# Sums of blocks of w_down kept in HBM, and 20 of 44 groups of the down product by seven block products

## The chip, the cores and the metric

The kernel runs on one core of one Trainium2 chip. The metric is the device time of one execution in microseconds. The engines are named as the profile names them: PE (TensorE; PEld its weight loads), DVE (VectorE), ACT (ScalarE), POOL (GpSimd), SP (SyncE, which here issues nearly all loads). ACTq and SPq are the instruction queues of ACT and SP as issuers of DMAs.

## The reference

One block of a transformer on 256 rows (S) of 2048 columns (D), in float32: three kinds of attention side by side, gated and merged, then a feed-forward part with a short causal convolution.

```python
h = rms_norm(x, g_mix)
proj = h @ w_in                        # fq fk fv f_logit | sq sk sv | mq | gates
o_fox = forgetting_attention(...)      # 6 heads
o_sb = stick_breaking_attention(...)   # 6 heads
o_mem = memory_attention(...)          # 4 heads, keys and values from mem @ w_mem_kv
g = sigmoid(gates.reshape(b, s, 3, D) + b_gate)
merged = g[:, :, 0] * (o_fox @ w_br_fox) + g[:, :, 1] * (o_sb @ w_br_sb) + g[:, :, 2] * (o_mem @ w_br_mem)
x = x + merged @ w_out
h2 = rms_norm(x, g_ffn)
u = causal_depthwise_conv(h2 @ w_up, conv_w, conv_b)
u_gate, u_val = split(u, 2)            # 5632 columns each
x = x + (silu(u_gate) * u_val) @ w_down
```

The change concerns the last line, the product of a = silu(u_gate) * u_val (256 x 5632) with w_down (5632 x 2048).

## The kernel before

Every float32 operand of a product is split into a high part and a low part of the type that TensorE takes (hi by a cast on ACT, lo by a subtraction on DVE), and each product is three matmuls: high by high, low by high, high by low. Weights come in pieces of 128 x 1024 (512 KB): a load on SP's queue into a tile raw (four buffers, WBUFS), a cast into hi on ACT (L135, in the down stage L825), a subtraction into lo on DVE (L136, L826), four buffers each (SBUFS).

The stages, in order: keys and values of the memory; the projections by w_in, for the memory queries (mq), the forgetting heads (f0 to f4), the stick-breaking heads (s0 to s4); then for four blocks of 512 columns the three gates (g) and three branch products (b); the product by w_out (o, four blocks); the product by w_up with the convolution (u); the product by w_down (x and y). All but u and the down stage go through product (L150), which takes two k tiles at a time and calls tick (L99) after each two. Work of the heads and transposes is written as generators, put in a queue by later (L96); a tick steps up to two of them (WINDOW), and so the small work is written into the order between the pieces of the large products. The instructions' final order on each engine is set by a planner when the program is built, from this order and its own costs; only where keep_in_program_order is called is it kept as written. On the chip each engine and each queue then runs in order.

The down stage (L776 to L925) takes w_down in two halves of 1024 columns (nb = 0, 1; PIECE = 1024) and the 44 k tiles in 22 pairs p, so 44 groups. A group by eight (eight, L840; letter e in the plans) loads two pieces and makes eight block products of 128 rows by 512 columns: two k tiles, two row tiles t, two column halves n. A group by seven (seven, L855; letter s) makes seven block products out of sums, after Strassen and Winograd: sums of blocks of a, held in sf (FS1 to FS4, made by forms, L791, once per pair for both halves), and sums of blocks of the weights (T1 to T4). With b00, b01 the two halves of the first k tile's piece and b10, b11 those of the second, DVE makes T1 = b00 + b01, T3 = b11 + b01, T2 = T1 + b11, T4 = T2 + b10 (L860, L861, L865, L870). The products go to the accumulators X (four banks) and Y (four banks); gather (L878) adds the Y banks into the residual xres after the last group by seven of a half. Each half ends with the addition of X to xres and the store of the output (L924, L925).

The plans of before (L897) are "eeee" + "see" * 5 + "eee" for the first half and "eee" + "se" * 7 + "eeeee" for the second: 5 and 7 groups by seven, 12 in all. The groups by seven use pairs from 0 on, the others the pairs behind them. forms is called after groups by eight (L913). The pool dn (L776 to L783: tiles raw, ts) is opened at the first call of sums and takes the memory of the convolution's pool (uv.close), so its first user waits for the last convolution. load (L808) goes round six tiles: four of wp, one of dn, one of xt_pool (tag xu).

```python
def tick():
    while waiting and len(active) < WINDOW:
        active.append([waiting.popleft(), 0])
```

Of the kernel before, what the change touches and what calls it, by code (L numbers as in the profile page):

```python
# [40 lines left out]
def hybrid_block(  # L41
# [54 lines left out]
    def later(gen):  # L96
        waiting.append(gen)

    def tick():  # L99
        while waiting and len(active) < WINDOW:  # L100
            active.append([waiting.popleft(), 0])
        for a in list(active):
            if a[1] > 0:
                a[1] -= 1
                continue
            try:
                a[1] = next(a[0]) or 0
            except StopIteration:
                active.remove(a)
# [7 lines left out]
    def finish():  # L117
        while waiting or active:
            tick()
# [345 lines left out]


# [311 lines left out]
    def sums(name, tag="ts"):  # L778
# [4 lines left out]
        return dn[0].tile([P, 1024], F32, tag=tag, name=name)  # L783

    ov = out[0].rearrange("(t p) d -> p t d", p=P)
    dv = w_down[0].rearrange("(k p) n -> p k n", p=P)
    NF = 7
    FS2, FS4, FS3, FS1 = range(4)
    sf = xt_pool.tile([P, NF, 4, 2, P], F32R, tag="xt", name="sf")

    def forms(p):  # L791

        v = aT[:, 2 * p : 2 * p + 2, :].bitcast(F32).rearrange("p k (l t q) -> p k l t q", l=2, t=NT)
        w = sums(f"fw_{p}")
        d = w[:, :512].rearrange("p (f l q) -> p f l q", f=2, l=2)
        r = w[:, 512:].rearrange("p (f q) -> p f q", f=4)
        nc.vector.tensor_tensor(d[:, 0], v[:, 0, :, 0], v[:, 0, :, 1], ALU.subtract)
        nc.vector.tensor_tensor(d[:, 1], v[:, 1, :, 1], v[:, 0, :, 1], ALU.subtract)
        nc.vector.tensor_tensor(r[:, :2], v[:, :, 0, 0], v[:, :, 1, 0], ALU.add)
        nc.vector.tensor_tensor(r[:, 2:], d[:, :, 0], d[:, :, 1], ALU.add)  # L800
        nc.vector.scalar_tensor_tensor(r[:, FS2], r[:, FS1], -1.0, r[:, FS2], ALU.mult, ALU.subtract)
        nc.vector.tensor_tensor(r[:, FS4], r[:, FS4], r[:, FS2], ALU.add)
        nc.scalar.copy(sf[:, p, :, 0], r)
        nc.vector.tensor_tensor(sf[:, p, :, 1], r, sf[:, p, :, 0].bitcast(F32), ALU.subtract)
# [3 lines left out]
    def load(k, n0):  # L808
        name = f"raw_d{n0}_{k}"
        loads[0] += 1  # L810
        at = loads[0] % (WBUFS + 2) if loads[0] > 10 else 0
        if at < WBUFS:
            raw = wp.tile([P, PIECE], F32, tag="raw", name=name)
        elif at == WBUFS:
            raw = sums(name, "raw")
        else:
            raw = xt_pool.tile([P, PIECE], F32, tag="xu", name=name)
        nc.sync.dma_start(raw, dv[:, k, n0 : n0 + PIECE])
        return raw
# [17 lines left out]
    def f_of(p, f):  # L837
        return sf[:, p, f, 0], sf[:, p, f, 1]
# [16 lines left out]
    def seven(p, n0, X, Y, first, last):  # L855
        k0, k1 = 2 * p, 2 * p + 1
# [3 lines left out]
        nc.vector.tensor_tensor(t[:, :512], b00, b01, ALU.add)  # L860
        nc.vector.tensor_tensor(b01, b11, b01, ALU.add)  # L861
        B00, T3 = parts(raw0, f"d{n0}_{k0}")
        three(Y[0], *a_of(k0, 0), B00, first, last)
        three(Y[3], *f_of(p, FS3), T3, first, last)
        nc.vector.tensor_tensor(t[:, 512:], t[:, :512], b11, ALU.add)  # L865
# [4 lines left out]
        nc.vector.tensor_tensor(b10, t[:, 512:], b10, ALU.add)  # L870
        T1, T2 = parts(t, f"t_{n0}_{p}")
        three(Y[2], *f_of(p, FS1), T1, first, last)
        three(Y[1], *f_of(p, FS2), T2, first, last)
        (T4,) = parts(b10, f"t4_{n0}_{p}")
        three(X[1][0], *a_of(k1, 1), T4)
        tick()

    def gather(n0, Y):  # L878
# [3 lines left out]
        w = sums(f"e_{n0}")  # L882
# [14 lines left out]
    plans = ("eeee" + "see" * 5 + "eee", "eee" + "se" * 7 + "eeeee")  # L897
    formed = 0
    for nb, plan in enumerate(plans):
# [4 lines left out]
        for i, c in enumerate(plan):  # L904
            if c == "s":
                seven(s, n0, X, Y, s == 0, s == ns - 1)
# [50 lines left out]
```

## Time and profile before

| | |
|---|---|
| time, median of 3 runs | 1492.08 us (1490.9 to 1492.4) |
| the profiled execution: its own time | 1490.28 us |
| its span | 1488.6 us |
| DMA | 283.62 MB, mean 191 GB/s |
| q1 (SP's queue) | 280.26 MB, 62.2% of the 16 engines |
| q10 (ACT's queue) | 2.11 MB, 0.4% |
| stretch of the down stage in the span | from 1252.5 us to the end |

A row of a view by lines has: line of the kernel, engine, operation, names (out<-in), shapes, count, then busy time in us and mean ns of one, then the idle time of the engine just before these instructions with what ended it. A row of the timeline has: start in us, duration in us, engine, line, operation, names, shapes, count and, in brackets, idle time before it with its releaser. A row of a table of stretches has: the stretch, its length, then the busy time and count of PE, PEld, DVE, ACT, POOL, then the granted clock of TensorE as a share, the busy share of the 16 DMA engines and their GB/s. A row of waits has: who waited for whom, us in total, times, longest. A row of DMA issues has: names, queue, count, KB of each, median us from issue to landing. A matmul's duration is from its start to its modelled end, and the next one starts before that end.

### The profile page before, as it was taken

Reading aid. Unit: us, or ns where it says so; the run is one execution under the profiler, and the core shown is the slowest. Engines: PE = TensorE matmul, PEld = TensorE weight load, DVE = VectorE, ACT = ScalarE, POOL = GpSimd, SP = SyncE. Lnnn points to the kernel's source line nnn. Section 1 sums busy time; section 2 is a strip of 40 time slices with the busy share of each in tenths; the row PEclk is TensorE's granted clock in tenths of the full one; section 3 lists DMA queues with packets and bytes.
Section 4 is the critical chain, followed back from the end, with each engine's and each line's share of the span. In section 5 each row is a group of like instructions: output and inputs, shape, how many; then the busy total and the mean of one; then the engine's idle time right before and its main releaser. Section 6 shows DMA issues by size and latency. Waiting matters only on the chain.

```text
span 1488.6 us, 19873 instructions
## 1 busy us (share of the span) xinstructions
PE 1481.9 (100%) x7430; PEld 1254.8 (84%) x7430; DVE 1016.9 (68%) x1457; ACT 791.9 (53%) x1100; POOL 16.2 (1%) x46
## 2 busy tenths in 40 slices
PE   9999999999999999999999999999999999999998
PEld 7888888888888888888888888888888888888887
DVE  5766566555655646556557778777778777898885
ACT  6755454458544444444456556556556556454552
POOL 0000000001000000000000000000000000000000
PEclk9999999999999999999999999999999999999999
DMA  9675475474666666655566666666666666666663
GB/s 309 200 200 159 125 224 157 119 223 152 192 196 207 190 206 203 185 192 189 185 179 182 204 186 184 197 187 183 199 194 185 194 189 197 192 206 217 214 205 114
DMA packets 138814, 283.62 MB, mean 191 GB/s; under 512 B 9290, under 2 KB 18398, under 8 KB 138718
## 3 DMA queue, kind: packets, MB, share of 16 engines
q1 hardware_dynamic: 137390, 280.26, 62.2%
q10 hardware_dynamic: 1328, 2.11, 0.4%
q8 instruction: 58, 0.95, 0.3%
q14 instruction: 38, 0.31, 0.1%
HBM read 280.23 MB, written 2.10 MB: 190 GB/s over the span
## 4 chain that ended last, share of the span: by engine, by line
PE 97%; ACT 1%; DVE 1%; POOL 0%; issue 0%; DMA 0%; SPq 0%; DVEq 0%; POOLq 0%
PE u L762 22%; PE u L763 11%; PE g L146 5%; PE g L148 5%; PE g L147 5%; PE x L832 4%; PE x L831 4%; PE x L830 4%; PE s L146 2%; PE s L148 2%; PE s L147 2%; PE f L146 2%; PE f L148 2%; PE f L147 2%; PE o L147 2%; PE o L148 2%
## 5 line engine op out<-in xcount | busy, mean ns | idle before, releaser
L762 PE MATMUL u<-hT,hi_u 128*128 128x512 f32 x1232 | 428.4, 391 | 0.0
L763 PE MATMUL u<-hT,lo_u 128*128 128x256 f32 x1232 | 345.0, 280 | 0.0
L136 DVE TENSOR_TENSOR lo_u<-raw_u,hi_u 128x1024 fp32r<-128x1024 f32 x176 | 215.4, 1224 | 115.2 <-ACT hi_u L135 115.1
L762 PEld LDWEIGHTS u<-hT,hi_u 128*128 128x128 f32 x1232 | 230.4, 187 | 50.5
L135 ACT CAST hi_u<-raw_u 128x1024 fp32r<-128x1024 f32 x176 | 184.8, 1050 | 139.0 <-PE u L762 112.6
L763 PEld LDWEIGHTS u<-hT,lo_u 128*128 128x128 f32 x1232 | 232.8, 189 | 0.0
L136 DVE TENSOR_TENSOR lo_g<-raw_g,hi_g 128x1024 fp32r<-128x1024 f32 x96 | 117.6, 1228 | 104.8 <-ACT hi_g L135 102.2
L135 ACT CAST hi_g<-raw_g 128x1024 fp32r<-128x1024 f32 x96 | 100.8, 1052 | 130.7 <-PE g L147 107.2
L146 PE MATMUL g<-hi_g,xT 128*128 128x512 f32 x336 | 132.2, 393 | 0.0
L148 PE MATMUL g<-lo_g,xT 128*128 128x512 f32 x336 | 131.0, 390 | 0.0
L147 PE MATMUL g<-hi_g,xT 128*128 128x512 f32 x336 | 130.8, 389 | 0.0
L825 ACT CAST hi_d<-raw_d 128x1024 fp32r<-128x1024 f32 x88 | 90.0, 1051 | 64.2 <-PE x L831 29.2
L826 DVE TENSOR_TENSOR lo_d<-raw_d,hi_d 128x1024 fp32r<-128x1024 f32 x88 | 105.8, 1222 | 21.6 <-ACT hi_d L825 19.9
L832 PE MATMUL x<-lo_d,aT 128*128 128x512 f32 x268 | 104.3, 390 | 0.1
L831 PE MATMUL x<-hi_d,aT 128*128 128x512 f32 x268 | 104.3, 389 | 0.0
L830 PE MATMUL x<-hi_d,aT 128*128 128x512 f32 x268 | 104.3, 389 | 0.0
L148 PEld LDWEIGHTS g<-lo_g,xT 128*128 128x128 f32 x336 | 63.1, 188 | 13.4
L147 PEld LDWEIGHTS g<-hi_g,xT 128*128 128x128 f32 x336 | 63.1, 188 | 12.7
L146 PEld LDWEIGHTS g<-hi_g,xT 128*128 128x128 f32 x336 | 63.1, 188 | 12.7
L136 DVE TENSOR_TENSOR lo_s<-raw_s,hi_s 128x1024 fp32r<-128x1024 f32 (+1 forms) x40 | 44.7, 1118 | 37.1 <-ACT hi_s L135 37.1
L136 DVE TENSOR_TENSOR lo_f<-raw_f,hi_f 128x1024 fp32r<-128x1024 f32 (+1 forms) x40 | 44.7, 1119 | 34.5 <-ACT hi_f L135 33.0
L135 ACT CAST hi_f<-raw_f 128x1024 fp32r<-128x1024 f32 (+1 forms) x40 | 38.6, 968 | 52.4 <-PE f L147 47.6
(358 smaller groups left out, 2797.4 us busy)
## 6 DMA issues: line engine op xcount, KB each, us to landing
raw_u<-in_w_up_dram SPq DMA_DIRECT2D x176, 512.0 KB, 4.2
raw_g<-in_w_in_dram SPq DMA_DIRECT2D x96, 512.0 KB, 3.7
raw_d<-in_w_down_dram SPq DMA_DIRECT2D x88, 512.0 KB, 5.0
raw_f<-in_w_in_dram SPq DMA_DIRECT2D x32, 512.0 KB, 3.7
raw_s<-in_w_in_dram SPq DMA_DIRECT2D x32, 512.0 KB, 3.7
raw_o<-in_w_out_dram SPq DMA_DIRECT2D x32, 512.0 KB, 4.3
raw_kv<-in_w_mem_kv_dram SPq DMA_DIRECT2D x15, 512.0 KB, 5.0
raw_b<-in_w_br_fox_dram SPq DMA_DIRECT2D x12, 512.0 KB, 4.8
```

The source lines that it names most:

```text
L135: pin(nc.scalar.copy(hi[:, :m], raw[:, :m]))
L136: pin(nc.vector.tensor_tensor(lo[:, :m], raw[:, :m], hi[:, :m].bitcast(F32), ALU.subtract))
L146: pin(nc.tensor.matmul(o, lhsT=xh, rhs=wh, start=first, stop=False))
L147: pin(nc.tensor.matmul(o, lhsT=xl, rhs=wh, start=False, stop=False))
L148: pin(nc.tensor.matmul(o, lhsT=xh, rhs=wl, start=False, stop=last))
L762: nc.tensor.matmul(ps[i], lhsT=hi[:, j, c], rhs=hT(k + j), start=first, stop=False)
L763: nc.tensor.matmul(ps[i][:, :S], lhsT=lo[:, j, c], rhs=hT(k + j)[:, :S], start=False, stop=last)
L825: nc.scalar.copy(hi[:, :n], src)
L826: nc.vector.tensor_tensor(lo[:, :n], src, hi[:, :n].bitcast(F32), ALU.subtract)
L830: nc.tensor.matmul(o, lhsT=ah, rhs=w[0], start=first, stop=False)
L831: nc.tensor.matmul(o, lhsT=al, rhs=w[0], start=False, stop=False)
L832: nc.tensor.matmul(o, lhsT=ah, rhs=w[1], start=False, stop=last)
```

## The change

Twenty groups are done by seven products, ten in each half. Their weight sums T1 to T4 are no longer made in the down stage: a generator weight_sums makes them from the stage of the memory queries on and stores them in 20 tiles in HBM (kept, 128 x 4 x 512 float32, 1 MB each). It is stepped once by every tick outside finish. For each tile it works in two halves of 256 columns: two loads of 256 KB on ACT's queue into a tile pre (one buffer), two steps on, three DVE operations (one of 128 x 512, two of 128 x 256), one step on a store of 512 KB on ACT's queue, and two steps more. A half so takes five steps, all of it 200.

seven now loads five blocks on SP's queue: b00 and T3 into one raw tile, the second k tile's piece into another, T1 and T2 into a third, T4 into a tile of sm (tag junk, two buffers). It has no sums on DVE any more. forms is called where the plan has an f; it has four sums on DVE (one of 512 columns, one of 256, two of 128), two casts on ACT and two differences on DVE. FS1 is stored in aT, in the place of the block of a that no product needs any longer; sf holds the other three, 28 in its main tile and two in a tile of dn.

```diff
-    def tick():
+    background = []
+
+    def tick(beside=True):
+        if beside and background:
+            next(background[0], None)
@@
     def finish():
         while waiting or active:
-            tick()
+            tick(beside=False)
@@
+    plans = ("efefeff" + "ssef" * 2 + "sseff" * 2 + "sseeeee", "ee" + "sse" * 5 + "eeeee")
+    dram = ctx.enter_context(tc.tile_pool(name="dram", bufs=1, space=bass.MemoryType.DRAM))
+    dv = w_down[0].rearrange("(k p) n -> p k n", p=P)
+    T1, T3, T4, T2 = range(4)
+    sums_of = {}
+
+    def weight_sums(pool):
+        for nb, plan in enumerate(plans):
+            for p in range(plan.count("s")):
+                kept = dram.tile([P, 4, 512], F32, tag=f"kept_{nb}_{p}", name=f"kept_{nb}_{p}")
+                for h in range(2):
+                    w = pool.tile([P, 4, 256], F32, tag="pre", bufs=1, name=f"pre_{nb}_{p}_{h}")
+                    n0 = nb * PIECE + h * 256
+                    for n in range(2):
+                        nc.scalar.dma_start(
+                            w.rearrange("p (k n) c -> p k n c", k=2)[:, :, n],
+                            dv[:, 2 * p : 2 * p + 2, n0 + n * 512 : n0 + n * 512 + 256],
+                        )
+                    yield
+                    yield
+
+                    both = w[:, 1:2].to_broadcast([P, 2, 256])
+                    nc.vector.tensor_tensor(w[:, 0:2], w[:, 0:4:3], both, ALU.add)
+                    nc.vector.tensor_tensor(w[:, T2], w[:, T1], w[:, T2], ALU.add)
+                    nc.vector.tensor_tensor(w[:, T4], w[:, T2], w[:, T4], ALU.add)
+                    yield
+                    nc.scalar.dma_start(kept[:, :, h * 256 : (h + 1) * 256], w)
+                    yield
+                    yield
+                sums_of[nb, p] = kept
@@ behind weighted, ahead of the projection of the memory queries
+    background.append(weight_sums(gp))
@@ behind the product by w_out
+    assert next(background.pop(), None) is None
     mix.close()
@@ forms
-        nc.vector.tensor_tensor(d[:, 0], v[:, 0, :, 0], v[:, 0, :, 1], ALU.subtract)
-        nc.vector.tensor_tensor(d[:, 1], v[:, 1, :, 1], v[:, 0, :, 1], ALU.subtract)
-        nc.vector.tensor_tensor(r[:, :2], v[:, :, 0, 0], v[:, :, 1, 0], ALU.add)
-        nc.vector.tensor_tensor(r[:, 2:], d[:, :, 0], d[:, :, 1], ALU.add)
-        nc.vector.scalar_tensor_tensor(r[:, FS2], r[:, FS1], -1.0, r[:, FS2], ALU.mult, ALU.subtract)
-        nc.vector.tensor_tensor(r[:, FS4], r[:, FS4], r[:, FS2], ALU.add)
-        nc.scalar.copy(sf[:, p, :, 0], r)
-        nc.vector.tensor_tensor(sf[:, p, :, 1], r, sf[:, p, :, 0].bitcast(F32), ALU.subtract)
+        nc.vector.tensor_tensor(w[:, :512].rearrange("p (k c) -> p k c", k=2), v[:, :, 0], v[:, :, 1], ALU.add)
+
+        a10 = w[:, P : 2 * P].unsqueeze(1).to_broadcast([P, 2, P])
+        nc.vector.tensor_tensor(r[:, FS3 : FS1 + 1], w[:, :512].rearrange("p (f q) -> p f q", f=4)[:, 0:4:3], a10, ALU.subtract)
+        nc.vector.scalar_tensor_tensor(r[:, FS2], r[:, FS1], -1.0, a[:, 0, 0], ALU.mult, ALU.subtract)
+        nc.vector.tensor_tensor(r[:, FS4], r[:, FS2], a[:, 1, 0], ALU.add)
+        at = 3 * p
+        if at + 3 <= NX:
+            groups = [(sf[:, at : at + 3], r[:, :3])]
+        else:
+            groups = [(s_of(p, f), r[:, f]) for f in range(3)]
+        groups.append((s_of(p, FS1), r[:, FS1]))
+        for dst, src in groups:
+            nc.scalar.copy(dst[..., 0, :], src)
+        for dst, src in groups:
+            nc.vector.tensor_tensor(dst[..., 1, :], src, dst[..., 0, :].bitcast(F32), ALU.subtract)
@@ seven
-        raw0, raw1 = load(k0, n0), load(k1, n0)
-        t = sums(f"t_{n0}_{p}")
-        b00, b01, b10, b11 = raw0[:, :512], raw0[:, 512:], raw1[:, :512], raw1[:, 512:]
-        nc.vector.tensor_tensor(t[:, :512], b00, b01, ALU.add)
-        nc.vector.tensor_tensor(b01, b11, b01, ALU.add)
+        kept = sums_of[nb, p]
+        raw0 = raw_tile(f"raw_d{n0}_{k0}")
+        nc.sync.dma_start(raw0[:, :512], dv[:, k0, n0 : n0 + 512])
+        nc.sync.dma_start(raw0[:, 512:], kept[:, T3])
+        raw1 = load(k1, n0)
+        raw2 = raw_tile(f"raw_t{n0}_{p}")
+        nc.sync.dma_start(raw2.rearrange("p (n c) -> p n c", n=2), kept[:, 0:4:3])
+        raw3 = sm.tile([P, 512], F32, tag="junk", bufs=2, name=f"raw_t4_{n0}_{p}")
+        nc.sync.dma_start(raw3, kept[:, T4])
@@
-        nc.vector.tensor_tensor(t[:, 512:], t[:, :512], b11, ALU.add)
@@
-        nc.vector.tensor_tensor(b10, t[:, 512:], b10, ALU.add)
-        T1, T2 = parts(t, f"t_{n0}_{p}")
+        T1w, T2w = parts(raw2, f"t_{n0}_{p}")
@@
-    plans = ("eeee" + "see" * 5 + "eee", "eee" + "se" * 7 + "eeeee")
@@ the loop over a plan
+            elif c == "f":
+                forms(formed)
+                formed += 1
             else:
                 eight(e, n0, X, i == 0, i == len(plan) - 1)
                 e += 1
-                if e >= 2 and s < ns and formed <= (s if nb == 0 else ns - 1):
-                    forms(formed)
-                    formed += 1
```

More of the change, by code (lines that the diff above doesn't have):

```diff
@@ L776, in hybrid_block, with place @@
     dn = []
-    def sums(name, tag="ts"):
+    def place(shape, dt, tag, name):
         if not dn:
@@ new lines, in hybrid_block, with s_of @@
+    NX = 28
+    sf = xt_pool.tile([P, NX, 2, P], F32R, tag="xt", name="sf")
+    sf_rest = []
+    def s_of(p, f):
+        if f == FS1:
+            return aT[:, 2 * p].rearrange("p (l t q) -> p l t q", l=2, t=NT)[:, :, 1]
+        at = 3 * p + f
+        return sf[:, at] if at < NX else sf_rest[0][:, at - NX]
+    def forms(p):
+        if 3 * p + 3 > NX and not sf_rest:
+            sf_rest.append(place([P, 2, 2, P], F32R, "rest", "sf_rest"))
+        v = aT[:, 2 * p : 2 * p + 2, :].bitcast(F32).rearrange("p k (l c) -> p k l c", l=2)
+        w = place([P, PIECE], F32, "ts", f"fw_{p}")
+        a = w[:, :512].rearrange("p (k t q) -> p k t q", k=2, t=NT)
+        r = w[:, 512:].rearrange("p (f q) -> p f q", f=4)
+        nc.vector.tensor_tensor(w[:, :512].rearrange("p (k c) -> p k c", k=2), v[:, :, 0], v[:, :, 1], ALU.add)
[13 more added lines that the diff above has]
+            nc.vector.tensor_tensor(dst[..., 1, :], src, dst[..., 0, :].bitcast(F32), ALU.subtract)
@@ L806, in hybrid_block, with raw_tile @@
     loads = [0]
-    def load(k, n0):
-        name = f"raw_d{n0}_{k}"
+    def raw_tile(name):
         loads[0] += 1
@@ L812, in load @@
         if at < WBUFS:
-            raw = wp.tile([P, PIECE], F32, tag="raw", name=name)
+            return wp.tile([P, PIECE], F32, tag="raw", name=name)
         elif at == WBUFS:
-            raw = sums(name, "raw")
-        else:
-            raw = xt_pool.tile([P, PIECE], F32, tag="xu", name=name)
+            return place([P, PIECE], F32, "raw", name)
+        return xt_pool.tile([P, PIECE], F32, tag="xu", name=name)
+    def load(k, n0):
+        raw = raw_tile(f"raw_d{n0}_{k}")
         nc.sync.dma_start(raw, dv[:, k, n0 : n0 + PIECE])
@@ L869, in seven @@
         tick()
-        nc.vector.tensor_tensor(b10, t[:, 512:], b10, ALU.add)
-        T1, T2 = parts(t, f"t_{n0}_{p}")
[L872 to L875, printed above, removed]
+        T1w, T2w = parts(raw2, f"t_{n0}_{p}")
+        three(Y[2], *f_of(p, FS1), T1w, first, last)
+        three(Y[1], *f_of(p, FS2), T2w, first, last)
+        (T4w,) = parts(raw3, f"t4_{n0}_{p}")
+        three(X[1][0], *a_of(k1, 1), T4w)
         tick()
@@ L881, in gather @@
         xr = lambda t, n: xres[:, t, n0 + n * 512 : n0 + (n + 1) * 512]
-        w = sums(f"e_{n0}")
+        w = place([P, PIECE], F32, "ts", f"e_{n0}")
         e, f = w[:, :512], w[:, 512:]
```

22 lines of the change are left out of this document (9 added, 13 removed).

## Prediction

> **What bounds the kernel now.** First the page: busy shares and the chain of waits.
>
> ```profile
> PE 1481.9 (100%) x7430; PEld 1254.8 (84%) x7430; DVE 1016.9 (68%) x1457; ACT 791.9 (53%) x1100; POOL 16.2 (1%) x46
> ...
> PE 97%; ACT 1%; DVE 1%; POOL 0%; issue 0%; DMA 0%; SPq 0%; DVEq 0%; POOLq 0%
> ```
>
> The chain is TensorE for 97% of the span. A busy PE proves little, since matmuls overlap, so the next view is the timeline of PE in the down stage: its first matmul, the first group by seven, the group behind it, and the last matmul.
>
> ```profile
> 1252.49 0.39 PE L830 MATMUL x<-hi_d,aT 128*128 128x512 f32 x1
> ...
> 1274.29 0.39 PE L830 MATMUL y<-hi_d,aT 128*128 128x512 f32 x1
> ...
> 1279.28 0.39 PE L830 MATMUL x<-hi_d,aT 128*128 128x512 f32 x1
> ...
> 1484.20 0.39 PE L832 MATMUL x<-lo_d,aT 128*128 128x512 f32 x1
> ```
>
> Four groups by eight of 24 matmuls lie between the first two rows: 21.80 us / 96 = 0.2271 us for each (the 0.39 is a latency). The stage has 32 groups of 24 and 12 of 21, 1020 matmuls: 1020 x 0.2271 = 231.6 us. From 1252.49 to the last start and one matmul more are 231.9 us, so PE loses 0.3 us there, most of it in the first group by seven (4.99 us where 21 x 0.2271 = 4.77). The time of this stage is its count of matmuls. Whether that still holds with fewer depends on the other resources, by stretch (engines, clock, DMA share, GB/s):
>
> ```profile
> 10.00:20.00 10.00, 9.65 (x48) 7.81 (x49) 6.31 (x10) 6.06 (x12) 0.00 (x0) 1.00 1.04 381
> 340.00:690.00 350.00, 349.70 (x1571) 289.36 (x1570) 203.89 (x212) 166.76 (x172) 7.89 (x16) 1.00 0.65 192
> 1250.00:1480.00 230.00, 229.94 (x1017) 189.71 (x1016) 193.78 (x251) 116.82 (x131) 0.00 (x0) 1.00 0.59 195
> ```
>
> The clock is granted in full. In the down stage VectorE is busy 84% (193.78 of 230) and is the second limit. The DMA engines have moved 381 GB/s where they were asked to.
>
> **The change, part by part.**
>
> *Fewer products.* Eight more groups by seven, each without one product of three matmuls: 8 x 3 x 0.2271 = **-5.45 us** on the path that sets the end. The matmuls that stay have the same shapes. Nothing can gain more: the stage loses only 0.3 us.
>
> *VectorE in the down stage.* Durations by form:
>
> ```profile
> L826 DVE TENSOR_TENSOR lo_d<-raw_d,hi_d 128x1024 fp32r<-128x1024 f32 x83 | 99.7, 1222 | 16.9 <-ACT hi_d L825 15.2
> L860 DVE TENSOR_TENSOR t<-raw_d 128x512 f32<-128x512 f32 x12 | 8.3, 691 | 1.8 <-DMA raw_d<-in_w_down_dram 1.5
> L826 DVE TENSOR_TENSOR lo_t<-raw_d,hi_t 128x512 fp32r<-128x512 f32 x12 | 8.3, 688 | 1.5 <-ACT hi_t L825 1.5
> L804 DVE TENSOR_TENSOR sf<-fw,sf 128x512 fp32r<-128x512 f32 x7 | 4.8, 690 | 2.8 <-ACT sf L803 2.8
> L797 DVE TENSOR_TENSOR fw<-aT 128x256 f32<-128x256 f32 x7 | 3.0, 424 | 0.2
> L801 DVE SCALAR_TENSOR_TENSOR fw<-fw 128x128 f32<-128x128 f32 x7 | 2.0, 288 | 0.1
> ```
>
> A group by seven costs VectorE 3 x 1.22 + 0.69 + 4 sums of 0.69 = 7.1 us now and 4.35 us after, since the four sums come from HBM; a group by eight 2 x 1.22 = 2.44. A call of forms costs 4 x 0.42 + 2 x 0.29 + 0.69 = 2.95 now; after, 0.69 + 0.42 + 2 x 0.29, then differences over 384 and 128 columns (0.55 and 0.29, between the rows for 512 and 256, and as 128) = 2.53. Calls go from 7 to 10. A repeat "ss e f" then has 2 x 4.35 + 2.44 + 2.53 = 13.7 us of VectorE beside 66 x 0.2271 = 14.99 us of PE; "ss e ff" has 16.2, 1.2 us too much, in two repeats. Against that stands a lead:
>
> ```profile
> 1245.38 1.23 DVE L826 TENSOR_TENSOR lo_d<-raw_d,hi_d 128x1024 fp32r<-128x1024 f32 x1 [1.55 <-ACT hi_d L825]
> ...
> 1252.06 0.77 DVE L735 TENSOR_TENSOR cr<-cr,u 128x256 f32<-128x256 f32 x2
> ...
> 1266.75 0.43 DVE L168 TENSOR_TENSOR aT<-y,aT 128x256 fp32r<-128x256 f32 x1 [0.47 <-ACT aT L167]
> 1267.21 0.43 DVE L797 TENSOR_TENSOR fw<-aT 128x256 f32<-128x256 f32 x1
> ...
> 1269.00 0.29 DVE L802 TENSOR_TENSOR fw<-fw 128x128 f32<-128x128 f32 x1
> 1270.04 0.69 DVE L804 TENSOR_TENSOR sf<-fw,sf 128x512 fp32r<-128x512 f32 x1 [0.74 <-ACT sf L803]
> ...
> 1278.19 0.69 DVE L826 TENSOR_TENSOR lo_t<-raw_d,hi_t 128x512 fp32r<-128x512 f32 x1
> 1278.80 0.42 DVE L799 TENSOR_TENSOR fw<-aT 128x256 f32<-128x256 f32 x1
> 1279.14 2.36 DVE L826 TENSOR_TENSOR lo_d<-raw_d,hi_d 128x1024 fp32r<-128x1024 f32 x2
> ```
>
> The first lo_d is ready at 1246.61 and PE takes it at 1252.49: 5.9 us of lead, what four pairs of hi and lo buffers allow. It covers 2 x 1.2 us if regained between; bounds 0 and 2.4, I take **+0.5**.
>
> *The first group by seven comes earlier.* It stands behind three groups by eight, not four: at 1252.49 + 72 x 0.2271 = 1268.84, and its second product needs the low part of FS3 0.9 us later, at 1269.75. Forms can't start before the last convolution frees the memory of pool dn: 1266.75 + 0.43 = 1267.2 now, with VectorE full since 1252.06, and the same after, as nothing ahead of it changes. Of the first call the six sums took 2.1 us, the wait for ACT's copy 0.75, the difference 0.69; with 1.7 us of sums (some 1.55 as they overlap) and 0.55 it ends at 1270.06, 0.3 us late: the lower bound. Upper: four calls now stand ahead of that group, 10.1 us, and if VectorE did all four first, the parts of both groups that remain (1.22 + 0.69 + 4.35) would end at 1267.2 + 16.4 = 1283.6, where PE wants the last at 1268.84 + 42 x 0.2271 - 0.45 = 1277.9: 5.7 us. The last rows above show lo parts slipped in between the dependent operations of a call, so I take **+1.2**: 0.3 and most of one such part (1.22).
>
> *Sums made ahead.* 20 tiles of 1 MB in halves: 40 times two loads and a store on ACT's queue and three operations on VectorE (0.69 + 2 x 0.42 = 1.53 us; 61 us in all). A half takes 5 of the 248 ticks of the products; 200 are needed, so they end in the last quarter of the gates. A tick is 12 matmuls, 2.73 us.
>
> ```profile
> 408.31 1.05 ACT L135 CAST hi_g<-raw_g 128x1024 fp32r<-128x1024 f32 x1 [1.67 <-PE b L147]
> 448.47 1.23 DVE L136 TENSOR_TENSOR lo_g<-raw_g,hi_g 128x1024 fp32r<-128x1024 f32 x1 [1.50 <-ACT hi_g L135]
> L925 ACTq DMA_DIRECT2D out_dram<-xres x9: 338/338/445, 1367.0 to 1485.5; - x9
> raw_g<-in_w_in_dram SPq DMA_DIRECT2D x96, 512.0 KB, 3.7
> raw_d<-in_w_down_dram SPq DMA_DIRECT2D x88, 512.0 KB, 5.0
> ```
>
> Both engines idle over 1.5 us for each piece, 7.5 us in five ticks, against 1.53 us on VectorE and 3 x 0.338 = 1.0 us of issuing on ACT. Three waits are added. VectorE's sum waits for its load: behind it stand the lo parts. ACT's store waits for that sum, and its next load for the store, since tile pre has one buffer: behind both stand the hi casts. Each has two ticks, 5.5 us, or one; transfers of 512 KB land in 3.7 to 5.0 us. A wait that overruns by a microsecond falls into the 5.9 us of lead, which is the cover; without it each of 40 would cost its overrun. It is gone in one place:
>
> ```profile
> 334.00:352.00 18.00, 17.85 (x85) 14.68 (x84) 10.07 (x14) 16.69 (x21) 3.04 (x5) 1.00 0.50 149
> ...
> PEld r L626 <- POOL sb L603: 1.1, 2, 0.6
> ```
>
> Here a pair of stick-breaking heads keeps ACT busy 93%, and PE waits for its mask (0.15 us of idle PE in this window). A second pair does the same some 27 us later. Lower bound 0 if the issues fall outside, upper 7 us a pair (a rival below); I take **+0.4** for all of the stages ahead, one issue in each pair's stretch.
>
> *Traffic.* Ahead of the down stage 1.05 MB each five ticks (13.6 us), 77 GB/s on top of 192: at 192 / 0.65 = 295 GB/s for a full share that is 0.91, so it fits. In the down stage a group by seven reads 1.75 MB (1.835 million bytes), five blocks in rows of 2 KB, one of 4 KB, in 4.77 us: 385 GB/s; "ss e" 4.72 million bytes in 14.99 us, 315, below the 381 of the table. Eight buffers of raw pieces lie between. Taken: 0; upper bound with the rivals. SP's load of a T4 waits for the lo of the T4 two groups before, and the next weights stand behind it; that lies 10 us or more ahead, hence nothing. The stores of the sums ended some 600 us earlier.
>
> [...]
>
> **Sum.** -5.45 + 1.2 + 0.5 + 0.4 = -3.35 us. The profiled execution took 1490.28 (span 1488.6 and 1.7 around it), 1.8 under the median 1492.08; against the median: **1488.7 us**.
>
> **Rivals.** *Forms hold PE at the head of the down stage*: the upper bound 5.7 in place of 1.2 and 0.5 becomes 1.5: -5.45 + 5.7 + 1.5 + 0.4 = +2, or with half of it, -1: 1491 to 1494, no change. For it: VectorE full from 1252. Against: the lo parts slipped in.
>
> *DMA bounds the pairs.* At the full-share rates, 295 GB/s for rows of 2 KB and 195 / 0.59 = 331 for 4 KB, a seven takes 1.311 / 295 + 0.524 / 331 = 6.03 us and an eight 3.17, "ss e" 15.2 us against 15.0: nine times 0.2, and twice 1.3 where the buffers run dry, some 4 us: 1492. Against it: 381 GB/s at a share of 1.04, so that the share overstates. [...]
>
> *Slower: ACT's queue in the stretches of the stick-breaking heads.* A pair's stretch of 27 us holds two halves, six issues (2.0 us) and two waits of a store for sums (1.53 each, and about 1 of landing beyond two ticks): up to 7 us of ACT, on a chain that PE already waits for. At 5.2 us a pair: -5.45 + 1.7 + 10.4 = +6.7: 1498.7. It decides from 3.4 us a pair.
>
> *Slower: the DMA engines full at the gates.* If rows of 1 KB cost as much each as rows of 2 KB, a half takes 7.1 of its 13.6 us, 0.52 on top of 0.65: 17% too much over 112 ticks (305 us), +52 us. At half of that, in proportion to the bytes, it is 0.26 and all fits; it decides from some 4.8 us for a half, where 0.65 + 0.35 is 1.
>
> **How the numbers follow.** Forecast 0.43, forms 0.18, DMA in the pairs 0.10, ACT's queue 0.20, full engines 0.09. A measurement of this kernel tells 0.2%, 3 us, from no change. Faster: the forecast but for its upper end, 0.39. Same: that end and the two rivals about zero, 0.32. Slower: 0.29. The forecast's own range is 1486.8 (every cost at its lower bound, with 0.3 off) to 1490. The whole range reaches from 1486.3 to 1500, which leaves out the full engines and the worst of ACT's queue.
>
> **What would show it.** PE in the down stage: 996 matmuls, 226.2 us, with a gap of about a microsecond at the first group by seven, behind sf; small gaps at lo in "ss e ff". The raw loads there at some 270 GB/s, with no wait of ACT for a raw_d. In the stages ahead PE without new gaps but at L626. Wrong if PE waits for lo_g or hi_g in the gates, if DMA stands behind raw tiles in the pairs, or if the gap ahead of the first pair exceeds 3 us.

## The result, and the profile after

The changed kernel took 1557.37 us (median of four runs, 1555.95 to 1558.11) beside 1492.19 us for the kernel before (four runs, 1490.9 to 1492.4): a ratio of 1.0442 with a 95% interval of 1.0429 to 1.0455, 65 us slower. The profiled execution took 1556.67 us with a span of 1554.9, 66.3 us longer than the span before. The page of the changed kernel, busy shares, one queue and the chain of waits:

```profile
PE 1504.7 (97%) x7406; PEld 1262.5 (81%) x7406; DVE 1051.6 (68%) x1558; ACT 797.4 (51%) x1127; POOL 16.8 (1%) x46
...
q10 hardware_dynamic: 44208, 44.06, 8.4%
...
PE 69%; DMA 20%; DVE 5%; ACT 3%; issue 2%; ACTq 1%; DVEq 0%
```

PE has 24 matmuls fewer, as it should, and the chain is PE for only 69% of the span: 20% are transfers, which had 0%. ACT's queue (q10) moves 44 MB where it moved 2.11, which takes 8.4% of the DMA engines. Where the time lies shows from the starts of the stages in PE's timeline (first matmul to first matmul, us):

| stage | before | after | difference |
|---|---|---|---|
| keys and values of the memory, from 0 | 58.9 | 85.5 | +26.6 |
| memory queries | 22.9 | 22.9 | 0 |
| f, forgetting heads | 111.3 | 117.4 | +6.1 |
| s, stick-breaking heads | 113.8 | 125.3 | +11.5 |
| gates and branch products | 365.5 | 391.6 | +26.1 |
| product by w_out, product by w_up | 580.1 | 580.1 | 0 |
| down stage, to the end of its last matmul | 231.9 | 228.0 | -3.9 |

The down stage is 3.9 us shorter; everything lost is lost ahead of w_up, and 26.6 us of it in the first 85 us, ahead of the place where weight_sums is put on the list. Two views say why. The first is the table of stretches (columns as in the prediction), two rows of before and then four of after:

```profile
0.00:112.00 112.00, 109.66 (x514) 87.88 (x515) 74.40 (x124) 71.74 (x130) 1.51 (x10) 1.00 0.75 237
...
307.00:675.00 368.00, 367.70 (x1657) 304.68 (x1656) 215.16 (x227) 181.48 (x193) 11.02 (x24) 1.00 0.65 193
```

```profile
0.00:115.00 115.00, 96.06 (x405) 74.36 (x406) 64.51 (x115) 59.94 (x114) 1.50 (x10) 0.93 0.77 246
115.00:225.00 110.00, 106.86 (x526) 89.69 (x525) 75.28 (x133) 46.20 (x75) 0.00 (x0) 0.98 0.74 227
225.00:350.00 125.00, 119.16 (x587) 99.39 (x587) 79.79 (x147) 52.69 (x89) 3.56 (x12) 0.96 0.78 242
350.00:745.00 395.00, 377.88 (x1666) 307.83 (x1666) 235.12 (x273) 175.05 (x191) 11.77 (x24) 0.99 0.72 221
```

PE stands idle for 18.9, 3.1, 5.8 and 17.1 us there, 45 us together, against some 2.6 in both rows of before, and the granted clock is under 1. A finer table of stretches has twelve windows of 3.41 us at a clock of 0.50, 41 us, which cost about 19 us of work (an estimate: half of the 38 us that PE is busy in them). 42 of idle time and 19 of clock are 61 of the 70 us lost ahead of the down stage; the other 9 aren't told apart here. The second view is that of one tile, pre, in the changed kernel: each row has durations in ns (least, median, most) and the first and the last start in us; below, the waits, with us in total, times and the longest:

```profile
L223 ACTq DMA_DIRECT2D pre<-in_w_down_dram x80: 369/378/691, 1.3 to 534.7; - x80
L231 DVE TENSOR_TENSOR pre<-pre x40: 671/693/773, 7.0 to 539.7; 128x512 f32<-128x512 f32 x40
```

```profile
DVE pre L231 <- DMA pre<-in_w_down_dram: 78.5, 30, 7.1
...
ACT hi_g L139 <- DVE pre L233: 24.3, 6, 5.9
...
ACT sb L671 <- DMA kept<-pre: 12.3, 3, 5.0
...
PE kv L152 <- DVE lo_kv L140: 10.6, 4, 4.4
PE g L152 <- DVE lo_g L140: 10.6, 8, 3.3
```

The first load of pre is issued at 1.3 us, though the ticks that write it start with the memory queries: the planner has moved the sums' operations. VectorE then stands before 30 of the 40 sums until a load lands, 78.5 us in all, with the lo parts behind it; ACT stands at stores until the sums are made, with the hi casts behind it. One such cycle in the gates, in the timeline of ACT, DVE and PE:

```profile
495.10 0.90 ACTq L223 DMA_DIRECT2D pre<-in_w_down_dram  x2
...
498.03 1.98 ACT L139 CAST hi_g<-raw_g 128x1024 fp32r<-128x1024 f32 x2
505.24 0.53 ACTq L235 DMA_DIRECT2D kept<-pre  x1
505.88 1.05 ACT L139 CAST hi_g<-raw_g 128x1024 fp32r<-128x1024 f32 x1 [5.88 <-DVE pre L233]
510.39 0.90 ACTq L223 DMA_DIRECT2D pre<-in_w_down_dram  x2
511.41 2.00 ACT L139 CAST hi_g<-raw_g 128x1024 fp32r<-128x1024 f32 x2 [4.48 <-issue]
```

```profile
497.19 1.23 DVE L140 TENSOR_TENSOR lo_g<-raw_g,hi_g 128x1024 fp32r<-128x1024 f32 x1 [1.05 <-ACT hi_g L139]
502.58 0.69 DVE L231 TENSOR_TENSOR pre<-pre 128x512 f32<-128x512 f32 x1 [4.16 <-DMA pre<-in_w_down_dram]
```

```profile
501.20 0.39 PE L151 MATMUL g<-hi_g,xT 128*128 128x512 f32 x1
504.92 0.69 PE L152 MATMUL g<-lo_g,xT 128*128 128x512 f32 x1 [3.34 <-DVE lo_g L140]
505.41 0.63 PE L150 MATMUL g<-hi_g,xT 128*128 128x512 f32 x1
505.84 0.63 PE L151 MATMUL g<-hi_g,xT 128*128 128x512 f32 x1
```

The load is issued at 495.10. The first sum stands in DVE's order a single lo part later: 4.16 us idle. ACT has made two more hi casts and then stands 5.88 us at the store, whose sums aren't there. PE runs out of lo_g for 3.34 us, and when it goes on its matmuls are 0.43 us apart instead of 0.23, with the granted clock at 0.50 from 505.05 to 508.46. After the store ACT makes one hi cast and stands again, 4.48 us, at the next load. That load takes the one buffer of pre, which the store still reads, so the kernel makes it wait until the store has landed; the profile names no releaser here.

DVE does not pass its wait by: it idles 4.16 us though both hi_g of 498.03 are cast by 500.01, and their lo parts come at 503.65 and 505.12, behind the sum. The 5.88 and the 4.48 us are idle time of ACT itself, in front of its casts.

In the down stage the timeline of PE in the changed kernel (first matmul, first group by seven and its second half, last matmul) reads:

```profile
1322.75 0.39 PE L892 MATMUL x<-hi_d,aT 128*128 128x512 f32 x1
...
1342.22 0.50 PE L892 MATMUL y<-hi_d,aT 128*128 128x512 f32 x1 [0.82 <-ACT hi_d L887]
...
1346.87 0.50 PE L892 MATMUL y<-hi_t,aT 128*128 128x512 f32 x1 [0.41 <-ACT hi_t L887]
...
1550.57 0.39 PE L894 MATMUL x<-lo_d,aT 128*128 128x512 f32 x1
```

From 1322.75 to 1550.57 and one matmul more are 228.05 us; 996 matmuls at 0.2271 are 226.2. The first group by seven has two gaps of 0.82 and 0.41 us, and with what follows them loses 1.9 us; no other place loses over 0.15.

### The profile page after: what moved, and what is told of

The parts are those of the page before. It is cut to its first block, busy times and chain, and to the rows that moved or that the text cites. A ratio compares the mean times of both kernels' runs of the same rounds, so it can differ in the third digit from the quotient of the medians.

```text
span 1554.9 us, 20294 instructions
## 1 busy us (share of the span) xinstructions
PE 1504.7 (97%) x7406; PEld 1262.5 (81%) x7406; DVE 1051.6 (68%) x1558; ACT 797.4 (51%) x1127; POOL 16.8 (1%) x46
## 4 chain that ended last, share of the span: by engine, by line
PE 69%; DMA 20%; DVE 5%; ACT 3%; issue 2%; ACTq 1%; DVEq 0%
PE u L805 21%; PE u L806 11%; DMA kept<-pre 10%; DMA pre<-in_w_down_dram 9%; PE x L892 4%; PE x L893 4%; PE x L894 4%; PE g L152 3%; PE g L150 3%; PE g L151 3%; PE o L150 2%; PE o L152 2%; PE o L151 2%; PE b L152 1%; PE b L151 1%
## 5 line engine op out<-in xcount | busy, mean ns | idle before, releaser
L892 PE MATMUL x<-hi_d,aT 128*128 128x512 f32 x212 | 82.6, 390 | 0.0
L893 PE MATMUL x<-hi_d,aT 128*128 128x512 f32 x212 | 82.5, 389 | 0.0
L894 PE MATMUL x<-lo_d,aT 128*128 128x512 f32 x212 | 82.0, 389 | 0.0
L231 DVE TENSOR_TENSOR pre<-pre 128x512 f32<-128x512 f32 x40 | 27.8, 694 | 80.1 <-DMA pre<-in_w_down_dram 78.5
L139 ACT CAST hi_s<-raw_s 128x1024 fp32r<-128x1024 f32 (+1 forms) x40 | 38.0, 960 | 55.2 <-PE s L151 22.1
L140 DVE TENSOR_TENSOR lo_o<-raw_o,hi_o 128x1024 fp32r<-128x1024 f32 x32 | 39.2, 1225 | 36.8 <-ACT hi_o L139 32.3
```

Source lines behind the costliest of these rows:

```text
L139: pin(nc.scalar.copy(hi[:, :m], raw[:, :m]))
L140: pin(nc.vector.tensor_tensor(lo[:, :m], raw[:, :m], hi[:, :m].bitcast(F32), ALU.subtract))
L892: nc.tensor.matmul(o, lhsT=ah, rhs=w[0], start=first, stop=False)
L893: nc.tensor.matmul(o, lhsT=al, rhs=w[0], start=False, stop=False)
L894: nc.tensor.matmul(o, lhsT=ah, rhs=w[1], start=False, stop=last)
```

## The experiments

My theory after the result: what costs is neither the bytes nor the added operations, but engines with one order standing at transfers, because the planner put load, sum and store closer together than a transfer takes. Rivals: the traffic itself; the added work on ACT and DVE; the down stage. The kernel before took 1490.4 to 1490.9 us in the runs beside these experiments; ratios are to it.

**The two halves of the change, each alone.** In the first kernel the down stage is that of the change, but reads plain blocks of w_down of the same sizes; the sums T1 to T4 are left out.

```diff
-    background.append(weight_sums(gp))
@@ seven
-        nc.sync.dma_start(raw0[:, 512:], kept[:, T3])
+        nc.sync.dma_start(raw0[:, 512:], dv[:, k0, n0 + 512 : n0 + 1024])
```

> weight_sums is left out; the down stage of the changed kernel reads blocks of w_down of the same sizes in place of the kept sums (the sums T1 to T4 are left out). If the down stage gives what its matmuls say less its stalls (5.45 - 1.7), the time is 1487 to 1489.5 us with a down stage of 228 us. If part of the loss lies in the down stage, by its 35 percent more traffic, it is above 1492 us.

1487.14 us, ratio 0.9976 (0.9966 to 0.9985): 3.6 us faster. The second has weight_sums of the change and the down stage of before, which makes its own sums:

> weight_sums as in the changed kernel, with nobody reading the sums; down stage of the kernel before. If the whole loss stands ahead of the w_up stage: 1558 to 1564 us, 69 us above the kernel before. If it takes both parts together, under 1540 us.

1563.11 us, ratio 1.0483 (1.0462 to 1.0504). So the down stage brings what it was forecast to bring, and the whole loss lies in weight_sums.

**The order.** The operations of weight_sums are kept where the ticks write them:

```diff
+    keep = tc.keep_in_program_order
-                        nc.scalar.dma_start(
+                        keep(nc.scalar.dma_start(
@@ and the same around its three sums and its store
```

> Every operation of weight_sums is kept in the written order of its engine; traffic, sums and the down stage are those of the changed kernel. If the planner's moving them to the head of the queues, with ACT and DVE standing at transfers that land later than planned, is the cause, most of the 65 us go: 1488 to 1500 us, the first stage 59 us long again, no wait of DVE for pre over 3 us. If the 42 MB of added traffic starve the weight loads whatever the order, the time stays above 1530 us.

1503.08 us, ratio 1.0087 (1.0072 to 1.0102): 54 of the 65 us are gone, and the first stage takes 59.2 us, where it took 58.9 before and 85.5 in the change. But 16 us are left against the down stage alone, and the time lies 3 us above the expected range. In the waits of DVE and PE in this kernel, and in PE's timeline where a pair of stick-breaking heads runs:

```profile
DVE pre L233 <- DMA pre<-in_w_down_dram: 15.5, 9, 3.0
```

```profile
PE r L669 <- POOL sb L647: 3.7, 2, 1.9
PE fa L599 <- DVE fx L594: 2.1, 1, 2.1
PE tpm L533 <- DVE sm L498: 1.9, 2, 1.6
```

```profile
358.50 0.70 PE L669 MATMUL r<-sb,after 128*128 128x256 f32 x2 [1.90 <-POOL sb L647]
359.73 0.80 PE L670 MATMUL r<-sb,ones 128*128 128x128 f32 x2 [0.53 <-POOL sb L647]
```

A second pair has the same gaps some 31 us later (1.85 and 0.53). Behind the first the granted clock is 0.51 from 359.4 to 362.8 us, and its mean from 300 to 400 us, where both pairs lie, is 0.97. PE's waits for weights are small, 0.6 us for lo_f and 0.5 for lo_kv (0.5 before). What it waits for are tiles of the heads: of the memory heads (tpm), which run beside the stage f, of the forgetting heads (fa) beside s, of the stick-breaking heads (r) in the gates. These three stages are 4.6, 2.6 and 8.1 us longer than before.

With only ACT's loads and stores kept in order, and the three sums free:

> Only ACT's loads and stores of weight_sums are kept in the written order; the three sums on DVE may be moved. If it is ACT's queue that blocks, the time is that of the run with all kept, within 3 us. If DVE's standing at its load blocks too, the sums are still put right behind the planned landing and the time lies 5 us or more above that run.

1510.9 us, ratio 1.0142 (1.0121 to 1.0162), DVE's wait for the loads 49.1 us: 7.8 us more than with all of it kept. With the order free again, but weight_sums written in only behind the stick-breaking heads:

```diff
-    background.append(weight_sums(gp))
@@ the first block of gates, behind the heads
+            background.append(weight_sums(gp))
```

> weight_sums is written into the order only after the stick-breaking heads (what is left is drained ahead of the w_up stage), and nothing keeps its operations there. If the planner takes them forward to wherever their buffer is free, whatever the ticks say, the first load still stands at the head of ACT's queue and the time is above 1530 us. If the ticks' place counts, it is 1500 us or less.

1559.09 us, ratio 1.0462 (1.0432 to 1.0493): as the change itself. Its first load again is one of the first instructions on ACT. Where the unpinned work was written didn't count here.

**The traffic.** The fixed order, but the three sums left out, and stores of the same size that read rows of xres and so wait for no load:

```diff
-                    keep(nc.vector.tensor_tensor(w[:, 0:2], w[:, 0:4:3], both, ALU.add))
@@ the other two sums likewise
-                    keep(nc.scalar.dma_start(kept[:, :, h * 256 : (h + 1) * 256], w))
+                    keep(nc.scalar.dma_start(kept[:, :, h * 256 : (h + 1) * 256], xres[:, 0, :1024].rearrange("p (f c) -> p f c", f=4)))
```

> All kept in the written order, but the three sums on DVE are left out and the stores read rows of the residual: the same bytes in the same sizes at the same ticks, and no wait between loads, sums and stores but that of one load for the one before. If the 13 us by which the run with all kept is above the kernel before, in spite of the shorter down stage, come from waits in the queues, it is 1487 to 1491 us. If the traffic costs them, it stays at 1500 to 1504 us.

1488.2 us, ratio 0.9985 (0.9976 to 0.9994): the same bytes, queue and ticks cost 1 us over the down stage alone. The 15 us between this and the fixed order are the sums and what stands at them.

**The stick-breaking heads.** The fixed order, not stepped while the first block of gates runs, where these heads lie:

```diff
@@ around the first block of gates
+    held = background.pop()
...
+            background.append(held)
```

> All kept in the written order, and weight_sums is not stepped in the gates of the first block, where the stick-breaking heads run. If ACT's queue in their stretches is a part of the 16 us over the down-only run, as the rival of the prediction has it, the two gaps of 2.4 us at the heads' r matmuls and the two half-clock stretches behind them go: 1494 to 1498 us. If it is nothing, 1503 us again.

1495.56 us, ratio 1.0038 (1.0025 to 1.0051): 7.5 us less, with both pairs of gaps gone. 8.4 us over the down stage alone were left. They lie in f and s, 3.8 and 4.7 us longer than before, where PE waits 1.9 us for tpm and 3.0 for fa. The gates take 365.6 us beside 365.5 before: away from the heads two ticks of room are enough.

**Four ticks for a half: a miss.** weight_sums only in products without heads, what is left of it written in one piece ahead of w_up, and four steps for a half instead of five, by one step fewer between a store and the next load:

```diff
                     keep(nc.scalar.dma_start(kept[:, :, h * 256 : (h + 1) * 256], w))
                     yield
-                    yield
```

> All kept in the written order; weight_sums is stepped only in the products beside which no heads run (memory queries, first forgetting projection, and from the branch products of the first block on), four steps a half in place of five, the rest drained ahead of the w_up stage. If all that is left of the loss lies beside the heads, the stages ahead take what they took before and the time is 1487 to 1489.5 us, below both kernels. If 320 GB/s in the gates starve the weight loads, it is above 1495 us.

1546.1 us, ratio 1.0364 (1.0339 to 1.0388), far slower. ACT's timeline shows what the step was for:

```profile
639.86 0.52 ACTq L237 DMA_DIRECT2D kept<-pre  x1
640.50 1.05 ACT L139 CAST hi_g<-raw_g 128x1024 fp32r<-128x1024 f32 x1 [0.44 <-ACT hi_g L139]
645.34 0.90 ACTq L225 DMA_DIRECT2D pre<-in_w_down_dram  x2
646.36 2.00 ACT L139 CAST hi_g<-raw_g 128x1024 fp32r<-128x1024 f32 x2 [4.80 <-issue]
```

ACT stands 4.80 us ahead of the load. The profile names no releaser, but the load takes the one buffer that the store of 639.86 reads, and it goes out 5.5 us behind that store, about as long as such stores take to land (where POOL issues the loads, in an experiment below, the profile does name the store: 160.4 us in 39 waits):

```profile
kept<-pre ACTq DMA_DIRECT2D x40, 512.0 KB, 5.0
```

(a row of DMA issues of the change). In the gates this kernel takes 390.2 us where the one before it took 365.6, and PE waits 8.0 us for lo_g, so one tick less brings a standstill that the fixed order alone did not have. The traffic isn't the cause there: from 465 to 697 us this kernel moves 260 to 271 GB/s, and the kernel with the fixed order alone moves 277 GB/s from 500 to 600 us with PE full. But the step is only a part: the products by w_out and w_up take 613.7 us instead of 580.1, and the sums written ahead of w_up run beside them until 831 us.

**Another queue: a miss.** Loads and stores are issued by POOL, which is nearly idle (16.8 us busy in the change), so that ACT stands at nothing:

```diff
-                        nc.scalar.dma_start(
+                        nc.gpsimd.dma_start(
@@ the store likewise
```

With the change's free order, with the fixed order, and with the fixed order and the pause:

> As the changed kernel, nothing kept in order, but the loads and stores of weight_sums are issued from POOL's queue: ACT no longer stands at their waits, DVE's sums still stand right behind the planned landing. If ACT's standing is the larger part of the 69 us ahead of the w_up stage, 1500 to 1530 us; if DVE's standing at its loads is enough by itself (78.5 us of it in the changed kernel), 1540 us or more.

> All kept in the written order, loads and stores from POOL's queue. Of the 16 us over the down-only run those that ACT's queue costs go: 1490 to 1495 us, if POOL's masks of the heads are not held up behind these waits. If they are, the gaps at the r matmuls stay or grow and it is 1500 us or more.

> As the run before it, and weight_sums is not stepped in the gates of the first block. ACT and POOL free beside the stick-breaking heads: 1488 to 1490 us, below the kernel before by some 0.1 percent, if DVE's waits at its loads (two ticks of room) stay within its lead. Above 1493 us if those waits cost by themselves.

1619.72 us (1.0862, 1.0844 to 1.088), 1527.04 (1.0246, 1.0232 to 1.026) and 1503.06 (1.0084, 1.007 to 1.0098): each slower than its twin on ACT's queue. The waits of the first:

```profile
POOL kept L235 <- DVE pre L233: 217.2, 34, 10.6
DVE pre L231 <- DMA pre<-in_w_down_dram: 186.1, 38, 8.2
```

DVE now stands 186 us at loads where it stood 78.5. ACT no longer stands at these transfers, and PE starves all the same: most of its waits are for DVE (14.6 us for lo_kv, 12.0 for lo_f, 8.3 for lo_g, 17.2 for the heads' fx), and 9.1 for masks from POOL, which now stands at loads and stores itself. That moving the wait off one engine left it on another fits the theory; why the wait grew isn't shown. The transfers explain little of it: with fixed order the loads land in 5.3 us from POOL's queue and 4.8 from ACT's (medians). SP's queue was not tried.

**Room.** The last four kernels settle what was left. weight_sums gets two buffers for pre (paid with a weight slot, 13 instead of 14), and its steps overlap: still one half in five ticks, but four ticks between load and sums, two between sums and store, and four between a store and the load that takes its buffer again. First with the pause of above:

```diff
-BLOCKS = 14
+BLOCKS = 13
@@ weight_sums
-                    w = pool.tile([P, 4, 256], F32, tag="pre", bufs=1, name=f"pre_{nb}_{p}_{h}")
+            held[i] = w = pool.tile([P, 4, 256], F32, tag="pre", bufs=2, name=f"pre_{nb}_{p}_{h}")
...
+        for t in range(5 * len(halves) + 2):
+            for what, at in ((begin, 0), (add, 4), (put, 6)):
+                i, r = divmod(t - at, 5)
+                if r == 0 and 0 <= i < len(halves):
+                    what(i)
+            yield
```

> The sums in the order in which they are written, not stepped beside the heads of the first gate block, and with two buffers, so that four ticks (some 11 us of gates) lie between load and sums and two between sums and store. If what is left in the kernel with the pause (1495.6 us, 8.4 above the down stage alone) is engines standing at transfers with two ticks of room, the sums cost what the bare traffic costs: 1487.5 to 1490 us, VectorE's wait for the loads under 3 us and no PE gap of over 1 us ahead of w_up. If it is the added 40 x 3 operations on VectorE and their place in the splits' queue, 1493 to 1496 us as before. A slot fewer in the blocks of weights may cost by itself; the next kernel shows that.

1487.55 us, ratio 0.9979 (0.997 to 0.9987). The control, the kernel before with 13 slots:

> The kernel before with 13 instead of 14 weight slots, which is what the second buffer of the sums is paid with. If the slots are a reserve that nothing uses up, 1490 to 1493 us, as before; if a load comes late for want of a slot, PE shows gaps that the kernel before has not and the time is over 1494 us.

1490.9 us, ratio 1.0001 (0.9992 to 1.0011): the slot costs nothing. Without the pause:

> As the kernel with two buffers, but stepped beside the heads of the first gate block too. If the two gaps of the kernel with one buffer and fixed order (1.9 + 0.5 us each, each followed by a stretch at half clock) come from ACT standing at a store whose sums are late, they are gone with four ticks of room and the time is within 1.5 us of the kernel with the pause. If they come from the loads' and stores' issue and VectorE's added operations themselves in the heads' chain, both gaps are there again and the time is 4 to 8 us longer than with the pause.

1486.26 us, ratio 0.9969 (0.9958 to 0.998), the best of all kernels here, 4.6 us under the kernel before and level with the down stage alone. All of PE's waits in this kernel:

```profile
PE spare L90 <- DVE qscale L298: 1.2, 1, 1.2
PE y L907 <- ACT hi_d L902: 0.8, 1, 0.8
PE kv L152 <- DVE lo_kv L140: 0.5, 1, 0.5
PE y L907 <- ACT hi_t L902: 0.4, 1, 0.4
```

No wait for a mask, none in the gates, none of DVE for pre. The view of its tile pre and its stretch of the gates:

```profile
L235 DVE TENSOR_TENSOR pre<-pre x40: 680/684/771, 70.8 to 619.9; 128x512 f32<-128x512 f32 x40
...
DMA to landing us min/median/max: 3.0/5.5/7.5
```

```profile
307.00:675.00 368.00, 368.00 (x1661) 305.60 (x1661) 246.09 (x296) 182.59 (x195) 12.92 (x24) 1.00 0.82 261
```

The loads land in up to 7.5 us, where the longest of the change took 7.1, and it costs nothing: four ticks are 11 us. DVE carries 31 us more than before in this stretch, the DMA engines are at 0.82, and PE is full at full clock. Last, the same two buffers and the same steps, with the order free:

```diff
-    keep = tc.keep_in_program_order
+    keep = lambda x: x
```

> The kernel with two buffers and steps in every stage, with the operations of the sums free to be moved again. If two buffers alone make the room that was missing, it stays near the fixed one's 1486.3 us, under 1495. If the planner moves loads and sums ahead as it did with one buffer, the room written into the ticks is gone and VectorE and ACT stand at landings again: 1520 to 1565 us, VectorE's wait for the loads over 40 us and half-clock stretches behind PE's gaps.

1558.72 us, ratio 1.0454 (1.0437 to 1.0472). Its tile pre:

```profile
L235 DVE TENSOR_TENSOR pre<-pre x40: 676/692/694, 7.0 to 363.3; 128x512 f32<-128x512 f32 x40
```

The sums start at 7.0 us instead of 70.8 and end at 363 instead of 620, and DVE waits 69.5 us for loads. Room written into the steps is worth nothing where the order isn't kept; order without room leaves 16 us; both together leave none.

## Why the prediction was wrong

The time was missed by 68.7 us, in one term.

**Fewer products** (-5.45): 996 matmuls at the same interval, right.

**VectorE in the down stage** (+0.5) and **the first group by seven** (+1.2): the stage got shorter by 3.9 us in the trace, and the down stage alone was 3.6 us faster, where these three terms make -3.75. The first group lost 1.9 us where it had lost most of 0.3, so +1.6 for the 1.2, and the repeats "ss e ff" lost nothing of note. That the sum comes so close is in part luck: one term was 0.4 too small, the other 0.5 too large. Two details were off: the gap stands behind high parts from ACT (hi_d, hi_t), not behind sf; and the first call of forms began 16.3 us into the stage, not 14.7, because a lo part came ahead of the last convolution. The DMA engines moved 264 GB/s in this stage (forecast 270).

**Sums made ahead** (+0.4): this is the step that failed, and it took the place of the sum. It said "Each has two ticks, 5.5 us, or one" and "A wait that overruns by a microsecond falls into the 5.9 us of lead, which is the cover". The first takes the ticks for the order of the engines, although the section on the kernel says that a planner sets it and keeps what is written only where it is told to. The trace has the first load at 1.3 us and the sum behind one lo part; fixing the order took 54 us off. The second holds for the weights and fails for the heads. With the order fixed, two ticks still let DVE stand 15.5 us at nine loads, and the lead covered that in the products: PE waits 1.1 us for lo parts, 0.5 of which it waited before. But it waits 8.8 us for tiles of the heads, which have no such lead, and half clock follows (0.51 behind the first pair of gaps, 0.97 in the mean of the 100 us with both). "It is gone in one place" named the stick-breaking heads alone, and the memory and forgetting heads are two more such places; the three stages lose 15.3 us together, where +0.4 stood. I had set the two ticks against median landing times, where the longest (7.1 us in the change) decides for an engine that can't pass by. "Both engines idle over 1.5 us for each piece" was read from two single rows; the page of before has 130.7 us of idle time for 96 casts of hi_g and 104.8 for 96 of lo_g, 1.36 and 1.09 us each. It doesn't decide, since the cost of the work itself was rightly near nothing: with order and room, the sums add no time that can be measured to the down stage alone.

**Traffic** (0): right. The same bytes cost 1 us, and the full-engine rival falls: in the kernel with two buffers the DMA engines are at 0.82 in the gates, where 0.91 was worked out, with PE full.

**The rivals.** ACT's queue beside the stick-breaking heads was a real cost, but of the kernel with fixed order: the pause took 7.5 us off, 3.8 a pair where the rival had 5.2. It was a case of the same missing room, since four ticks and two buffers remove it without a pause. In the change itself it is buried under larger waits. Forms holding PE and DMA bounding the pairs did not occur: no wait of PE for a raw tile, no gap over 0.82 us.

**What would show it.** "Wrong if PE waits for lo_g or hi_g in the gates": it does, 10.6 us for lo_g.

## What to carry to other kernels

Work that is slipped in beside a full engine costs by where it stands in each in-order queue, not by its sum of durations: 61 us of DVE and 42 MB cost nothing when every sum stood 11 us behind its load and every store 5.5 us behind its sums, and most of 65 us when they stood an instruction or two behind. Before such work is priced at its written place, find out whether anything keeps it there; then give each wait more room than the longest landing in the trace, with a second buffer so that a store doesn't hold the next load. A lead of buffered weights covers short waits of the products only: look for small chains beside them that have no lead. And a gap on PE of two microseconds is to be priced with the half-clock stretch that can follow it: here 3.41 us at a clock of 0.50, up to 1.7 us more.

## What the runs showed of the hardware

In the changed kernel the granted clock fell to 0.50 behind short gaps of PE, for stretches of 3.41 us. Windows of that length, with PE's busy time as the first figure behind the length and the granted clock as the third from the end:

```profile
351.45:354.86 3.41, 1.70 (x8) 1.18 (x7) 3.28 (x4) 2.01 (x4) 0.00 (x0) 1.00 0.54 178
423.13:426.54 3.41, 0.87 (x4) 0.38 (x2) 1.57 (x4) 3.40 (x5) 0.00 (x0) 1.00 0.59 196
426.54:429.96 3.42, 3.03 (x9) 2.36 (x10) 3.42 (x4) 1.64 (x2) 2.99 (x4) 0.50 0.16 29
525.53:528.94 3.41, 1.24 (x6) 0.77 (x5) 2.75 (x5) 0.11 (x1) 0.00 (x0) 1.00 0.28 93
528.94:532.36 3.42, 3.42 (x10) 2.64 (x9) 2.21 (x2) 1.05 (x1) 0.00 (x0) 0.50 0.90 282
539.18:542.60 3.42, 1.81 (x9) 1.20 (x8) 2.68 (x4) 0.64 (x1) 0.00 (x0) 1.00 0.48 158
542.60:546.01 3.41, 3.41 (x16) 2.80 (x17) 2.96 (x3) 2.32 (x3) 0.00 (x0) 1.00 1.02 274
```

A whole window at half clock stands behind a window with 2.54 or 2.17 us of idle PE, none behind one with 1.61. The starts of the half-clock windows, 426.54 and 528.94, are 30 windows of 3.413 us apart, and the others in this trace fit the same grid; of ten windows with 1.85 us idle or more nine were followed by half clock (the tenth, from 6.71 us with 3.14, was not), of the windows at full clock with 1.71 or less none. In this trace the half clock went with the idle time of a whole window of the grid, not with one gap: a wait of 1.32 us that ended at 230.15 stood in a window with 1.85 us idle, and half clock followed; one of 1.71 us that ended at 353.47 was all that its window had, and none followed. A half-clock window costs up to 1.7 us, half of its length (an estimate: matmuls 0.43 us apart there, 0.23 elsewhere), and behind three of the nine stood a second one.

Loads issued from POOL's queue made DVE wait longer (119.5 us against 15.5 in fixed order), against what I had expected of an idle engine. The issue of one took 0.72 us there and 0.38 on ACT.
